# Second layer of an encoder: key and query weights, output-row squares, key spread and key scale at earlier places

## The chip, the core and the metric

The kernel runs on one core of a Trainium2 chip. The metric is the device time of one execution in microseconds (us), the median of several runs. The core has five engines that run side by side: PE (matrix products), DVE (vector work), ACT (activations and copies), POOL and SP. POOL and SP here mostly issue transfers: POOL those that convert or add on the way, SP plain ones.

## What is computed

A two-layer encoder over 1024 tokens of width 1024. In each layer a head group of latent attention runs beside a gated depthwise convolution of 31 taps; then comes a gated feed-forward block. The part that matters here:

```python
h = _rmsnorm(x, g_mix[l]);  p = h @ w_in[l]
c_q  = _rmsnorm(p[..., :384], g_q[l]);       q  = c_q @ w_uq[l]
c_kv = _rmsnorm(p[..., 384:640], g_kv[l]);   kv = c_kv @ w_ukv[l]
k_rope = _apply_rope(p[..., 640:672], cos, sin)
y_attn = _mla_attention(q_nope, q_rope, k_nope, k_rope, v)
u = a * sigmoid(gt);  u = _dwconv(u, w_dw_conv[l], b_dw_conv[l])
```

## The kernel before, in words

Everything is held transposed, 128 channels by 1024 tokens. A float32 factor is split into an upper and a lower part, and a product is made of three matmuls per half of the tokens (`product`, L252). `project` (L587) makes a layer's projections in sections: per section one block of 128 outputs in one of three wide places of PSUM. In the second layer the order is g0, a0, g1 (`next_sections`), then a1, g2, a2, g3, a3 (the convolution's gates), kv0, kv1 (key latent), kr (shared rope key), q0, q1, q2 (query latent), k0 to k3 (keys), u0, u1 (rope queries), n0 to n3 (queries).

The order on each engine is the order in which this code is written out; nothing is reordered later. `project` keeps a planned clock: `supply` (L922) asks for weights by the section's planned time, `out_squares` (L610) for rows of the output weights and their sum of squares, `work` (L635) emits queued steps of DVE and ACT, convolution taps among them, while the planned clock of DVE allows it. `start` (L665) emits a step's first part at once and queues the rest 1.8 us later on the planned clock.

Names that are needed below. `wk`, `wu2`, `wu0`, `wu1` are the weights of keys and queries, each an upper half (`h`, a converting transfer of POOL, L210) and a lower half (`l`: ACT writes the negated upper half, L225, and POOL adds the source to it, L226). `wor` are the output rows (SP L1043, squares by ACT L617). `hsq` is the square sum of `wk`. `far` tiles are scaled copies of the gate (ACT L2162) that POOL's transfers add into the convolution sums `conv` (L2163). `kss` is the key latent's sum of squares; `rkv1t` its transposes, `rkv1y` its inverse root (DVE L312 to L320), `rkv1s` the spread of that over the partitions (PE L339), `rkv` its copy (ACT L727). `keys_norm` (L724) scales the latent `ckv` by it and splits it into `kvs`, upper halves by ACT, lower by DVE (L785, L787). `kt` is a matmul that sums `qk` over the partitions; `key_scale` (L623) makes the keys' power-of-two scale from it, and `key_rope_end` (L769) the scaled rope key `krs`, which SP writes to memory as `krd`. `krt` is the rope key before that (L746). `cqs` are the split query latents, `qss` their sum of squares, `rq1y` the inverse root of that, `ks` the split keys.

Most of these tiles come from one pool, tag `b`, with 31 places of 4 KB per partition. A new tile gets a place that an older one had, and its first writer waits until the older tile's last user is done; for a `far` tile that is the landing of POOL's transfer.

Of the kernel before, what the change touches and what calls it, by code (L numbers as in the profile page):

```python
# [61 lines left out]
LEAD, TURN = 33.0, 22.0  # L62
# [62 lines left out]
BLOCKS = ("g0", "a0", "g1", "a1", "g2", "a2", "g3", "a3", "kv0", "kv1", "kr", "q0", "q1", "q2")  # L125
# [21 lines left out]
class Encoder:  # L147
# [102 lines left out]
                                           op0=ALU.mult, op1=ALU.subtract)  # L250
        return hi, lo

    def product(self, ps, weights, moving, by_half=False):
        nc = self.nc
        n = len(moving)
        for halves in ((0,), (1,)) if by_half else ((0, 1),):
            for k in range(n):
                (wh, wl), (xh, xl) = weights(k), moving[k]
                rest = ((wl, xh), (wh, xl)) if n <= 3 else ((wh, xl), (wl, xh))
                for s, (w, x) in enumerate(((wh, xh), *rest)):  # L260
                    for c in halves:
                        nc.tensor.matmul(ps[:, HALVES[c]], w, x[:, HALVES[c]], start=(k == 0 and s == 0),  # L262
                                         stop=(k == n - 1 and s == 2))
# [324 lines left out]
    def project(self, l, carry):  # L588
        nc, a = self.nc, self.a
        par = self.par[l]  # L590
        clock = {"pe": 0.0, "dve": 0.0}
        taps, active, u, conv, away, far_at = [], [], {}, {}, {}, {}
        gates, ckv, kvs, cq, cqs, vs, w = {}, [], [], [], [], [], {}
        heads, pending, spills = {}, {}, []
# [3 lines left out]
        krd = self.dp.tile([ROPE, 2, T], F16, name=f"krd{l}")  # L598
        qk = self.cp.tile([128, 8], F32, name=f"qk{l}", tag="qk", bufs=1)
        sc = self.cp.tile([128, 32], F32, name=f"sc{l}", tag="sc", bufs=1)  # L600
        outs = [(OUT_FROM + OUT_STEP * i, i, None) for i in range(4)]
        col = lambda i, n=1: qk[:, i:i + n]
        by = self.wz[:, 13:14]
        st = {}
# [18 lines left out]
        def key_scale():  # L623
            sums = self.bank(f"kt{l}", (128, 3))
            nc.tensor.matmul(sums, self.ones, col(4, 3), start=True, stop=True)
            nc.vector.tensor_copy(out=col(4, 3), in_=sums)
            nc.vector.scalar_tensor_tensor(out=col(4), in0=col(4), scalar=float(KVL), in1=col(5), op0=ALU.mult, op1=ALU.mult)
            nc.vector.tensor_tensor(out=col(4), in0=col(4), in1=col(6), op=ALU.add)
            self.half_exponent(col(5), col(4))
            self.power(col(6), col(5), -1.0, 200.0)  # L630
            self.power(col(2), col(5), 1.0, 54.0)
            nc.vector.tensor_scalar(out=col(2), in0=col(2), scalar1=SCALE, scalar2=None, op0=ALU.mult)
            launch(key_rope_end())

        def work(until):  # L635
            while True:
# [18 lines left out]
        def launch(steps, n=-1):  # L655
            active.append([clock["pe"], steps, n])
# [5 lines left out]
                    e[0] = clock["dve"] + step[1]  # L662
                active.remove(e)

        def start(steps):  # L665
            next(steps)
            active.append([clock["pe"] + 1.8, steps, 99])

        def gate(j):
            g = gates[j] = self.blk(f"gate{l}_{j}")  # L670
# [53 lines left out]
        def keys_norm():  # L724
            r = st["rkv"] = self.blk(f"rkv{l}")
            for s, p in zip(HALVES, self.spread(rooted("kroot"), f"rkv{l}", HALVES, self.bank)):
                nc.scalar.copy(out=r[:, s], in_=p)  # L727
            yield 0.0, 1.8
            for j in range(2):
                nc.vector.tensor_tensor(out=ckv[j], in0=ckv[j], in1=r, op=ALU.mult)  # L730
                yield 1.25, 0.0
            both = [parts(ckv[j], f"kvs{l}_{j}", kvs, par[:, P_GKV + j:P_GKV + j + 1]) for j in range(2)]
            yield [next(p) for p in both][0]
            for p in both:
                yield from p
# [34 lines left out]
        def key_rope_end():  # L770
            t, hl = st.pop("kr"), self.blk(f"krs{l}", F16, (128, 2, T))[0:32]
            by = qk[0:32, 6:7]
            nc.scalar.activation(out=hl[:, 0], in_=t, func=AF.Copy, scale=by)
            yield 0.0, 1.5
            nc.vector.scalar_tensor_tensor(out=hl[:, 1], in0=t, scalar=by, in1=hl[:, 0], op0=ALU.mult, op1=ALU.subtract)
            self.move(krd, hl)
            yield 1.25, 0.0

        def query_latent(j):
            yield from latent(f"q{j}", cq, "qss", j)  # L780
            yield from parts(cq[j], f"cqs{l}_{j}", cqs, par[:, P_GQ + j:P_GQ + j + 1])
# [70 lines left out]

        def inputs(name):
            if l:
                return lambda: self.product(ps[name], lambda k: (w[name][:, 0, k], w[name][:, 1, k]), hl)
            return lambda: self.product(ps[name], self.tiled(w[name]), hl)

        def ranked(group, j, n, name, moving):
# [5 lines left out]
        def root(key, out, n, name):  # L864
            ps = self.turned(st.pop(key), f"{name}{l}", HALVES, self.bank)

            def steps():
                st[out] = self.roots(ps, 8, n, f"{name}{l}")
                yield 2.5, 0.0

            pending[out] = [clock["pe"] + 2.0, steps(), 99]
            active.insert(0, pending[out])

        def rooted(out):
# [8 lines left out]
        add = lambda name, weight, emit, evict, after=None: seq.append((name, weight, emit, evict, after))  # L883
# [10 lines left out]
            add(f"kv{j}", f"kv{j}", inputs(f"kv{j}"), lambda j=j: latent(f"kv{j}", ckv, "kss", j))  # L894
        add("kr", "kr", shared_key, key_rope)
        add("q0", "q0", inputs("q0"), lambda: query_latent(0), lambda: root("kss", "kroot", KVL, "rkv"))
        add("q1", "q1", inputs("q1"), lambda: query_latent(1), lambda: (start(keys_norm()), key_scale()))
        add("q2", "q2", inputs("q2"), lambda: query_latent(2))
        between = {2 + l: lambda: root("qss", "qroot", QL, "rq")}
        norm = lambda: start(queries_norm())  # L900
# [15 lines left out]
        coming, turning = list(starts.items()) + [("v", t + 5.0)], []  # L916

        def rest_of(e):
            self.scaled_rest(*e)
            yield 1.28, 0.0  # L920

        def supply(now, turn=TURN):  # L922
            while coming and coming[0][1] <= now + LEAD:
                name, at = coming.pop(0)
                turning.append((name, at, self.cast(l, name)))
            while turning and turning[0][1] <= now + turn:
                name, at, e = turning.pop(0)
                if l and name in BLOCKS:
                    e = self.scaled(*e)
                    w[name] = e[0]  # L930
                    launch(rest_of(e), st.get("n", -3) - 2)
                    continue
                w[name] = self.complete(*e)
                if name == "k":
                    head_squares(name)

        hl, rx, ps = self.first_sections(l, supply) if l == 0 else self.next_sections(l, carry, supply)
# [146 lines left out]
    def wo_steps(self, l, conv, ys, w, casts, x, steps, put):  # L1084
# [14 lines left out]
        def load(i):  # L1099
            casts[i] = self.out_rows(l, i, "ws")  # L1100
# [1220 lines left out]
```

## Time and profile before

| | |
|---|---|
| median of 3 runs | 2173.98 us (2173.74 to 2175.91) |
| profiled execution | 2174.71 us, its span 2172.9 us |
| PE busy | 2160.1 us, 99% of the span |
| DVE, ACT, POOL busy | 86%, 68%, 24% |
| granted clock of PE, mean | 0.999 |

The profile is of one execution. Its span runs from the first instruction to the last; 1.8 us of the time lie outside. Times in rows are in us from the span's start. An engine takes its instructions strictly in order, so one that waits holds back all behind it. The sections of the change lie between 1140 and 1260 us.

### The profile page before, as it was taken

How to read it: one execution, taken by the hardware profiler on the slowest of the kernel's cores; microseconds unless marked ns; L12 is line 12 of the kernel's file. 1: busy time of each engine (PE TensorE's matmuls, PEld its weight loads, DVE VectorE, ACT ScalarE, POOL GpSimd, SP SyncE). 2: the span in 40 equal slices, each digit the busy share in tenths (PEclk: the TensorE clock that was granted, in tenths of full speed). 3: DMA queues.
4: the chain of work that ended last, by engine and by line, in shares of the span. 5: the costliest groups of instructions: out<-in, count | busy, mean ns of one | idle time of the engine just before them, and what ended most of it. 6: DMA issues, size and time to landing. Idle time of an engine off the chain costs nothing.

```text
span 2172.9 us, 29815 instructions
## 1 busy us (share of the span) xinstructions
PE 2160.1 (99%) x10726; PEld 1178.3 (54%) x10726; DVE 1859.4 (86%) x2558; ACT 1480.1 (68%) x2208; POOL 517.2 (24%) x506
## 2 busy tenths in 40 slices
PE   9999999999999999999999999999999999999998
PEld 8887666754444444444444576667544444444445
DVE  6989999879998887887978889998898988878877
ACT  6365888746898889554533768886478888865544
POOL 1232767211211111000000356771111111110000
PEclk9999999999999999999999999999999999999999
DMA  6898878854689898555334986786646988856533
GB/s 193 180 192 209 169 147 167 257 150 117 140 238 260 225 286 264 191 173 186 115 121 101 201 209 137 157 196 192 174 102 161 264 242 242 238 140 218 191 114 121
DMA packets 161220, 400.95 MB, mean 185 GB/s; under 512 B 19840, under 2 KB 27888, under 8 KB 161072
## 3 DMA queue, kind: packets, MB, share of 16 engines
q1 hardware_dynamic: 104080, 266.79, 35.8%
q0 software_dynamic: 56704, 131.74, 33.7%
q8 instruction: 84, 1.38, 0.3%
q10 hardware_dynamic: 288, 0.53, 0.1%
q14 instruction: 64, 0.52, 0.1%
HBM read 270.75 MB, written 69.66 MB: 157 GB/s over the span
## 4 chain that ended last, share of the span: by engine, by line
PE 93%; DVE 3%; ACT 2%; DMA 1%; issue 1%; DVEq 0%; SPq 0%; ACTq 0%
PE p L1376 36%; PE pd L1650 18%; PE po L1082 7%; PE s L1935 7%; PE t L1975 5%; PE pa L262 3%; PE o L1997 2%; PE pg L262 2%; PE pn L262 2%; PE pq L262 2%; PE pkv L262 1%; PE o L2002 1%; PE pg L585 1%; PE pv L1911 1%; PE pk L262 1%; DVE conv L2156 1%
## 5 line engine op out<-in xcount | busy, mean ns | idle before, releaser
L1376 PE MATMUL p<-b,w 128*128 128x512 f16 x3696 | 800.3, 379 | 0.3
L1376 PEld LDWEIGHTS <-w 128*128 128x128 f16 x3696 | 358.8, 98 | 431.7 <-issue 1.0
L1650 PE MATMUL pd<-ab,wd 128*128 128x512 f16 (+1 forms) x1920 | 401.0, 371 | 0.4 <-DVE ab L1640 0.4
L1252 POOL DMA_DIRECT2D wu<-in_w_up x176 | 152.5, 880 | 770.3 <-DVE w L1340 582.2
L1650 PEld LDWEIGHTS <-wd 128*128 128x128 f16 x1920 | 187.9, 98 | 210.7 <-issue 0.9
L1935 PE MATMUL s<-k,q 96*128 96x512 f16 x768 | 186.9, 379 | 0.0
L1340 DVE SCALAR_TENSOR_TENSOR w<-wu,wf,w 128x512 f16<-128x512 f32 (+1 forms) x216 | 177.3, 835 | 5.7 <-ACT w L1337 5.7
L1978 DVE SCALAR_TENSOR_TENSOR pt<-t,pt 128x512 f16<-128x512 f32 x256 | 163.0, 677 | 10.0 <-ACT pt L1977 9.0
L1337 ACT ACTIVATE w<-wu,wf 128x512 f16<-128x512 f32 (+1 forms) x216 | 165.2, 783 | 0.4 <-DMA wu<-in_w_up 0.4
L1977 ACT ACTIVATE pt<-t 128x512 f16<-128x512 f32 x256 | 139.2, 596 | 32.0 <-PE t L1975 30.0
L1937 DVE TENSOR_REDUCE mx<-s 128x1 f32<-128x1024 f32 x128 | 155.0, 1211 | 1.0 <-PE s L1935 1.0
L1639 ACT ACTIVATE ab<-ac,ds 128x512 f16<-128x512 f32 x108 | 75.6, 718 | 110.6 <-DVE ac L1545 73.6
L1945 ACT ACTIVATE p<-s,mx 128x1024 f32<-128x1024 f32 x128 | 143.3, 1120 | 2.3 <-DVE mx L1937 1.8
L2173 POOL TENSOR_SCALAR late<-gate,par 128x1012 f32<-128x1012 f32 (+14 forms) x99 | 135.8, 1372 | 27.4 <-PE pn L262 27.4
L2156 DVE SCALAR_TENSOR_TENSOR conv<-gate,par,conv 128x1009 f32<-128x1009 f32 (+14 forms) x110 | 139.7, 1274 | 2.8 <-ACT conv L688 0.2
L1975 PE MATMUL t<-ident,p 128*128 128x128 f32 x1024 | 136.6, 275 | 0.9 <-ACT p L1945 0.6
L1975 PEld LDWEIGHTS t<-ident,p 128*128 128x128 f32 x1024 | 116.8, 141 | 34.9 <-issue 8.2
L1883 DVE SCALAR_TENSOR_TENSOR o<-zg,par,o 128x1023 f32<-128x1023 f32 x88 | 112.8, 1282 | 10.0 <-ACT o L1877 8.4
L1883 DVE SCALAR_TENSOR_TENSOR v<-zv,par,v 128x1023 f32<-128x1023 f32 x88 | 112.2, 1277 | 1.4 <-ACT v L1877 1.4
L1384 DVE SCALAR_TENSOR_TENSOR zg<-p,wf,zg 128x512 f32<-128x512 f32 x72 | 54.0, 750 | 66.3 <-PE p L1376 52.7
L2163 POOL DMA_DIRECT2D conv<-far x31 | 26.5, 867 | 351.2 <-ACT far L2162 332.2
L1935 PEld LDWEIGHTS <-q 96*128 96x128 f16 x768 | 74.1, 97 | 64.5 <-issue 2.1
(1536 smaller groups left out, 3710.9 us busy)
## 6 DMA issues: line engine op xcount, KB each, us to landing
wu<-in_w_up SPq DMA_DIRECT2D x98, 512.0 KB
wu<-in_w_up POOLq DMA_DIRECT2D x176, 256.0 KB, 5.1
sd<-in_w_down SPq DMA_DIRECT2D x44, 512.0 KB
ws<-sd SPq DMA_DIRECT2D x44, 512.0 KB
act<-v SPq DMA_DIRECT2D x36, 512.0 KB
ac<-act SPq DMA_DIRECT2D x72, 256.0 KB
wo<-in_w_o POOLq DMA_DIRECT2D x32, 256.0 KB, 7.9
x_mix<-y SPq DMA_DIRECT2D x32, 256.0 KB
```

Source lines behind the costliest of these rows:

```text
L262: nc.tensor.matmul(ps[:, HALVES[c]], w, x[:, HALVES[c]], start=(k == 0 and s == 0), stop=(k == n - 1 and s == 2))
L1252: nc.gpsimd.dma_start(out=dst, in_=src, accum_op=ALU.add)
L1337: nc.scalar.activation(out=t, in_=src, func=AF.Copy, scale=scale[f])
L1340: nc.vector.scalar_tensor_tensor(out=t, in0=src, scalar=scale[f], in1=hi, op0=ALU.mult, op1=ALU.subtract)
L1376: nc.tensor.matmul(ps, w[p][:, k * 128:(k + 1) * 128], b[:, q], start=(i in (1, 5, 2) and k == 0 and t == 0), stop=(k == 3 and t == 2), sk ...
L1650: nc.tensor.matmul(ps[t, m][:, cs], w[i, j][p][:, m * 128:(m + 1) * 128], b[:, q, cs], start=(i in (1, 5, 2) and j == 0 and s == 0), stop= ...
L1883: self.nc.vector.scalar_tensor_tensor(out=o[:, a:b], in0=z[:, at + a:at + b], scalar=self.par[l][:, tap:tap + 1], in1=o[:, a:b], op0=ALU.m ...
L1935: nc.tensor.matmul(ps[:, cs], q[0:96, i, qs], k[0:96, j, cs], start=(s == 0), stop=(s == 2))
L1937: nc.vector.tensor_reduce(out=mx, in_=ps, op=ALU.max, axis=AX.X, negate=True)
L1975: nc.tensor.transpose(tp[:, i, qi * 128:(qi + 1) * 128], st["p"][2 * qp + qi][:, kt * 128:(kt + 1) * 128], self.ident)
L1978: nc.vector.scalar_tensor_tensor(out=lo, in0=tp, scalar=P_SCALE, in1=hi, op0=ALU.mult, op1=ALU.subtract)
L2156: self.nc.vector.scalar_tensor_tensor(out=y[:, lo:hi], in0=u[:, lo + s:hi + s], scalar=self.tap(l, j, t), in1=y[:, lo:hi], op0=ALU.mult, o ...
```

## The change

All of it concerns the second layer. (1) `supply` asks for `wk` and the `wu` weights 40 us sooner than before, past names that are still in the queue, and the `wu` tiles come from the pool `b` instead of `ws`. (2) The output rows start at a planned time of 6 us instead of 56. (3) The spread of the keys' inverse root and the matmul `kt` are emitted inside the product of section q1, before its fifth and its eighth slice, instead of behind it; the steps that follow are queued. (4) The inverse root may be taken 0.5 us after its sums on the planned clock instead of 2.0.

```diff
--- before.py
+++ after.py
@@ -74,6 +74,7 @@
 END_TURNS = 1
 SCALES_AT = 2, 4.2
 OUT_FROM, OUT_STEP, OUT_WAIT = 56.0, 10.0, 24.0
+OUT_NEXT, AHEAD = 6.0, 40.0
 WO_LOAD = (0, 1, 2, 3)
 WO_UPPER = (3, 2), (3, 2.1), (4, 2), (5, 2)
 WO_LOWER = (3, 4), (4, 2), (5, 2), (6, 2)
@@ -250,11 +251,13 @@
                                            op0=ALU.mult, op1=ALU.subtract)
         return hi, lo
 
-    def product(self, ps, weights, moving, by_half=False):
+    def product(self, ps, weights, moving, by_half=False, between={}):
         nc = self.nc
         n = len(moving)
         for halves in ((0,), (1,)) if by_half else ((0, 1),):
             for k in range(n):
+                if k in between:
+                    between[k]()
                 (wh, wl), (xh, xl) = weights(k), moving[k]
                 rest = ((wl, xh), (wh, xl)) if n <= 3 else ((wh, xl), (wl, xh))
                 for s, (w, x) in enumerate(((wh, xh), *rest)):
@@ -598,7 +601,7 @@
         krd = self.dp.tile([ROPE, 2, T], F16, name=f"krd{l}")
         qk = self.cp.tile([128, 8], F32, name=f"qk{l}", tag="qk", bufs=1)
         sc = self.cp.tile([128, 32], F32, name=f"sc{l}", tag="sc", bufs=1)
-        outs = [(OUT_FROM + OUT_STEP * i, i, None) for i in range(4)]
+        outs = [((OUT_NEXT if l else OUT_FROM) + OUT_STEP * i, i, None) for i in range(4)]
         col = lambda i, n=1: qk[:, i:i + n]
         by = self.wz[:, 13:14]
         st = {}
@@ -623,6 +626,7 @@
         def key_scale():
             sums = self.bank(f"kt{l}", (128, 3))
             nc.tensor.matmul(sums, self.ones, col(4, 3), start=True, stop=True)
+            yield 0.0, 0.0
             nc.vector.tensor_copy(out=col(4, 3), in_=sums)
             nc.vector.scalar_tensor_tensor(out=col(4), in0=col(4), scalar=float(KVL), in1=col(5), op0=ALU.mult, op1=ALU.mult)
             nc.vector.tensor_tensor(out=col(4), in0=col(4), in1=col(6), op=ALU.add)
@@ -631,6 +635,7 @@
             self.power(col(2), col(5), 1.0, 54.0)
             nc.vector.tensor_scalar(out=col(2), in0=col(2), scalar1=SCALE, scalar2=None, op0=ALU.mult)
             launch(key_rope_end())
+            yield 1.2, 0.0
 
         def work(until):
             while True:
@@ -662,9 +667,9 @@
                     e[0] = clock["dve"] + step[1]
                 active.remove(e)
 
-        def start(steps):
+        def start(steps, wait=1.8):
             next(steps)
-            active.append([clock["pe"] + 1.8, steps, 99])
+            active.append([clock["pe"] + wait, steps, 99])
 
         def gate(j):
             g = gates[j] = self.blk(f"gate{l}_{j}")
@@ -852,7 +857,8 @@
 
         def inputs(name):
             if l:
-                return lambda: self.product(ps[name], lambda k: (w[name][:, 0, k], w[name][:, 1, k]), hl)
+                between = {4: lambda: start(keys_norm(), 6.5), 7: lambda: start(key_scale(), 9.6)} if name == "q1" else {}
+                return lambda: self.product(ps[name], lambda k: (w[name][:, 0, k], w[name][:, 1, k]), hl, between=between)
             return lambda: self.product(ps[name], self.tiled(w[name]), hl)
 
         def ranked(group, j, n, name, moving):
@@ -868,7 +874,7 @@
                 st[out] = self.roots(ps, 8, n, f"{name}{l}")
                 yield 2.5, 0.0
 
-            pending[out] = [clock["pe"] + 2.0, steps(), 99]
+            pending[out] = [clock["pe"] + (0.5 if l else 2.0), steps(), 99]
             active.insert(0, pending[out])
 
         def rooted(out):
@@ -894,7 +900,7 @@
             add(f"kv{j}", f"kv{j}", inputs(f"kv{j}"), lambda j=j: latent(f"kv{j}", ckv, "kss", j))
         add("kr", "kr", shared_key, key_rope)
         add("q0", "q0", inputs("q0"), lambda: query_latent(0), lambda: root("kss", "kroot", KVL, "rkv"))
-        add("q1", "q1", inputs("q1"), lambda: query_latent(1), lambda: (start(keys_norm()), key_scale()))
+        add("q1", "q1", inputs("q1"), lambda: query_latent(1), None if l else lambda: (start(keys_norm()), list(key_scale())))
         add("q2", "q2", inputs("q2"), lambda: query_latent(2))
         between = {2 + l: lambda: root("qss", "qroot", QL, "rq")}
         norm = lambda: start(queries_norm())
@@ -919,12 +925,14 @@
             self.scaled_rest(*e)
             yield 1.28, 0.0
 
+        ahead = lambda name: AHEAD if l and name[0] in "ku" and name not in BLOCKS else 0.0
+
         def supply(now, turn=TURN):
-            while coming and coming[0][1] <= now + LEAD:
-                name, at = coming.pop(0)
-                turning.append((name, at, self.cast(l, name)))
-            while turning and turning[0][1] <= now + turn:
-                name, at, e = turning.pop(0)
+            for name, at in [e for e in coming if e[1] <= now + LEAD + ahead(e[0])]:
+                coming.remove((name, at))
+                turning.append((name, at, self.cast(l, name, "b" if ahead(name) and name != "k" else "ws")))
+            for name, at, e in [e for e in turning if e[1] <= now + turn + ahead(e[0])]:
+                turning.remove((name, at, e))
                 if l and name in BLOCKS:
                     e = self.scaled(*e)
                     w[name] = e[0]
```

In the change's order a line number is one to eight higher than before (L218 is now L219, L2162 is L2170).

**First place: ACT ahead of the rope key.** On ACT around the sections kr and q0 there stood before:

```order
L218 ACTIVATE wq1s_10547<-wq11r_10471,wz_75 128x1024 [waits DMAHW2_49]
L2162 ACTIVATE far1_2_16_10584<-gate1_2_10257,par1_155 128x1023 [waits DMASW2_49]
L218 ACTIVATE wq2s_10594<-wq21r_10545,wz_75 128x1024 [waits DMAHW4_49,DVE_49]
L2162 ACTIVATE far1_0_17_10647<-gate1_0_10052,par1_155 128x1022 [waits DMASW3_49]
L2162 ACTIVATE far1_1_17_10650<-gate1_1_10114,par1_155 128x1022 [waits DVE_49]
L2162 ACTIVATE far1_2_17_10653<-gate1_2_10257,par1_155 128x1022 [waits DMASW4_49]
L751 ACTIVATE krt1_10657<-pkr1_10551,wz_75 64x1024 [waits PE_49]
L763 COPY krt21_10664<-krt1_10657 32x1024 [waits DMASW5_49,DVE_49,Activation_49]
L766 ACTIVATE krt21_10664,qk1_9838<-krt1_10657 32x1024 [waits DVE_49]
```

And now:

```order
L219 ACTIVATE wq1s_10575<-wq11r_10492,wz_75 128x1024 [waits DMAHW6_49]
L226 ACTIVATE wu01l_10495<-wu01h_10494 128x768 [waits DMASW6_49]
L2170 ACTIVATE far1_2_16_10612<-gate1_2_10261,par1_155 128x1023 [waits DVE_49]
L219 ACTIVATE wq2s_10619<-wq21r_10570,wz_75 128x1024 [waits DMAHW7_49,DMASW0_49]
L226 ACTIVATE wu11l_10573<-wu11h_10572 128x768 [waits DMASW2_49,PE_49]
L2170 ACTIVATE far1_0_17_10672<-gate1_0_10052,par1_155 128x1022 [waits DMASW1_49]
L2170 ACTIVATE far1_1_17_10675<-gate1_1_10114,par1_155 128x1022 [waits DMASW4_49,Activation_49]
L2170 ACTIVATE far1_2_17_10678<-gate1_2_10261,par1_155 128x1022 [waits DVE_49]
L756 ACTIVATE krt1_10682<-pkr1_10579,wz_75 64x1024 [waits DMASW6_49,Activation_49]
L768 COPY krt21_10689<-krt1_10682 32x1024 [waits DVE_49,PE_49]
```

POOL's transfers report on eight counters in turn, DMASW0 to DMASW7. On POOL there now stand, in order:

```order
L211 DMA wu11h_10572<-in_w_uq 128x2x384 [waits DMAHW3_49,DMAHW6_49,DMASW2_49,DVE_49]
L227 DMA wu01l_10495<-in_w_uq 128x2x384 [waits DMAHW7_49,DMASW3_49,Activation_49]
L2171 DMA conv1_2_10331<-far1_2_16_10612 128x1023 [waits DMAHW1_49,DVE_49,Activation_49]
L227 DMA wu11l_10573<-in_w_uq 128x2x384 [waits DMAHW5_49,Activation_49]
L2171 DMA conv1_0_10112<-far1_0_17_10672 128x1022 [waits DMASW6_49,DMASW0_49,Activation_49]
L2171 DMA conv1_1_10179<-far1_1_17_10675 128x1022 [waits DMASW7_49,DMASW1_49,Activation_49]
L2171 DMA conv1_2_10331<-far1_2_17_10678 128x1022 [waits DMASW4_49,Activation_49]
L2171 DMA conv1_0_10112<-far1_0_18_10785 128x1021 [waits DMASW6_49,Activation_49]
L2171 DMA conv1_1_10179<-far1_1_18_10788 128x1021 [waits DMASW7_49,DMASW2_49,Activation_49]
L2171 DMA conv1_2_10331<-far1_2_18_10791 128x1021 [waits DMASW3_49,DMASW0_49,Activation_49]
```

The lower halves of `wu0` and `wu1` stand between the far copies now. Counting from `wu11h`, whose landing ACT's `wu11l` awaits on DMASW2, the transfer of `far1_2_16` is DMASW4 and that of `far1_0_17` DMASW6. So `far1_1_17` now waits for the landing of `far1_2_16`, and `krt1`, which waited for PE before, for that of `far1_0_17`: `far1_1_17` has the place that `far1_2_16` had, `krt1` the place of `far1_0_17`.

**Second place: ACT behind the root's spread.** Before, from the far copies to the rope key's end:

```order
L2162 ACTIVATE far1_0_18_10742<-gate1_0_10052,par1_155 128x1021
L2162 ACTIVATE far1_1_18_10745<-gate1_1_10114,par1_155 128x1021 [waits PE_49]
L2162 ACTIVATE far1_2_18_10748<-gate1_2_10257,par1_155 128x1021 [waits DMASW1_49]
L785 ACTIVATE cqs1_0h_10751<-cq01_10679,par1_155 128x1024
L727 COPY rkv1_10772<-rkv1s_10773 128x512 [waits PE_49]
L727 COPY rkv1_10772<-rkv1s_10778 128x512 [waits PE_49]
L709 ACTIVATE cq11_10794<-pq11_10693,wz_75 128x1024 [waits Activation_49]
L719 ACTIVATE qss1_1_10796<-cq11_10794 128x1024 [waits Activation_49]
L225 ACTIVATE wu21l_10684<-wu21h_10683 128x768 [waits DMASW2_49]
L617 ACTIVATE wor1_1b_10549,sc1_9839<-wor1_1b_10549 128x1024 [waits DMAHW5_49]
L773 ACTIVATE krs1_10804<-krt1_10657,qk1_9838 32x1024 [waits DMASW4_49,DVE_49]
```

And now:

```order
L732 COPY rkv1_10733<-rkv1s_10747 128x512 [waits PE_49]
L732 COPY rkv1_10733<-rkv1s_10752 128x512 [waits PE_49]
L2170 ACTIVATE far1_0_18_10785<-gate1_0_10052,par1_155 128x1021 [waits DMASW0_49]
L2170 ACTIVATE far1_1_18_10788<-gate1_1_10114,par1_155 128x1021 [waits DMASW5_49]
L2170 ACTIVATE far1_2_18_10791<-gate1_2_10261,par1_155 128x1021
L790 ACTIVATE cqs1_0h_10794<-cq01_10704,par1_155 128x1024 [waits DMASW1_49,Activation_49]
L790 ACTIVATE kvs1_0h_10802<-ckv01_10488,par1_155 128x1024 [waits DMASW2_49,DVE_49,Activation_49]
L790 ACTIVATE kvs1_1h_10805<-ckv11_10566,par1_155 128x1024 [waits DVE_49,Activation_49]
L778 ACTIVATE krs1_10815<-krt1_10682,qk1_9838 32x1024 [waits DMASW3_49,DVE_49]
```

The spread's copies stand ahead of the far copies now, and the upper halves `kvs` ahead of `krs`. `cqs1_0h`, `kvs1_0h` and `krs1` wait for the landings of `far1_0_18`, `far1_1_18` and `far1_2_18` (DMASW1, 2 and 3).

**Third place: DVE from the rope key's end to the first keys.** Before:

```order
L775 SCALAR_TENSOR_TENSOR krs1_10804<-krt1_10657,qk1_9838,krs1_10804 32x1024 [waits DMASW4_49,DMASW0_49,Activation_49]
L730 TENSOR_TENSOR ckv01_10467<-ckv01_10467,rkv1_10772 128x1024
L730 TENSOR_TENSOR ckv11_10541<-ckv11_10541,rkv1_10772 128x1024
L280 SCALAR_TENSOR_TENSOR qss1_10681<-qss1_10681,qss1_1_10796 128x1024 [waits DMASW7_49,DMASW3_49]
L2156 SCALAR_TENSOR_TENSOR conv1_3_10459<-gate1_3_10389,par1_155,conv1_3_10459 128x1021
L787 SCALAR_TENSOR_TENSOR kvs1_0l_10869<-ckv01_10467,par1_155,kvs1_0h_10868 128x1024 [waits PE_49,Activation_49]
L787 SCALAR_TENSOR_TENSOR kvs1_1l_10872<-ckv11_10541,par1_155,kvs1_1h_10871 128x1024 [waits Activation_49]
L787 SCALAR_TENSOR_TENSOR cqs1_1l_10876<-cq11_10794,par1_155,cqs1_1h_10875 128x1024 [waits DMASW1_49,Activation_49]
L2156 SCALAR_TENSOR_TENSOR conv1_3_10459<-gate1_3_10389,par1_155,conv1_3_10459 128x1022 [waits DVE_49]
L799 SCALAR_TENSOR_TENSOR ks1_0_10922<-pk01_10892,qk1_9838,ks1_0_10922 128x1024 [waits Activation_49]
```

And now:

```order
L780 SCALAR_TENSOR_TENSOR krs1_10815<-krt1_10682,qk1_9838,krs1_10815 32x1024 [waits DMASW3_49,Activation_49]
L792 SCALAR_TENSOR_TENSOR kvs1_0l_10803<-ckv01_10488,par1_155,kvs1_0h_10802 128x1024 [waits DMAHW0_49,DVE_49]
L792 SCALAR_TENSOR_TENSOR kvs1_1l_10806<-ckv11_10566,par1_155,kvs1_1h_10805 128x1024 [waits PE_49]
L283 SCALAR_TENSOR_TENSOR qss1_10706<-qss1_10706,qss1_1_10819 128x1024 [waits DMASW4_49,Activation_49]
L2164 SCALAR_TENSOR_TENSOR conv1_3_10480<-gate1_3_10402,par1_155,conv1_3_10480 128x1019
L2164 SCALAR_TENSOR_TENSOR conv1_3_10480<-gate1_3_10402,par1_155,conv1_3_10480 128x1020 [waits DVE_49]
L792 SCALAR_TENSOR_TENSOR cqs1_1l_10885<-cq11_10817,par1_155,cqs1_1h_10884 128x1024 [waits Activation_49]
L2164 SCALAR_TENSOR_TENSOR conv1_3_10480<-gate1_3_10402,par1_155,conv1_3_10480 128x1021 [waits DVE_49]
L2164 SCALAR_TENSOR_TENSOR conv1_3_10480<-gate1_3_10402,par1_155,conv1_3_10480 128x1022 [waits DVE_49]
L804 SCALAR_TENSOR_TENSOR ks1_0_10924<-pk01_10894,qk1_9838,ks1_0_10924 128x1024 [waits DMASW5_49,Activation_49]
```

`kvs1_0l` now waits on DMAHW0, which is the landing of SP's `krd`, since it has the place of `krs1`. Between `kvs1_1l` and `ks1_0` there stand four taps of `conv1_3` and the addition to `qss`, where one tap stood.

## Rows read from the trace of the kernel before

**Rows 1.** The page, chain that ended last: shares of the span by engine
```profile
PE 93%; DVE 3%; ACT 2%; DMA 1%; issue 1%; DVEq 0%; SPq 0%; ACTq 0%
```

**Rows 2.** Who PE waited for in the whole run: us in total, times, longest
```profile
PE pk L262 <- DVE kvs_0l L787: 1.8, 1, 1.8
```

**Rows 3.** PE in order of time: start us, us, what [idle before]
```profile
1209.41 10.52 PE L262 MATMUL pq<-xs,wq1s 128*128 128x512 f16 x48
...
1221.83 0.38 PE L625 MATMUL kt<-qk,ones_r 128*128 128x3 f32 x2 [1.03 <-ACT rkv L727]
...
1235.62 0.73 PE L262 MATMUL pk<-kvs_0l,wk1h 128*128 128x512 f32 x2 [1.76 <-DVE kvs_0l L787]
...
1251.11 1.06 PE L339 MATMUL rq1s<-ident,rq1y 128*128 128x128 f32 x8 [0.26 <-DVE rq1y L317]
```

**Rows 4.** The chain in order of time: start us, us, what
```profile
1235.62 10.27 PE pk L262 x44
```

**Rows 5.** ACT in order of time
```profile
1195.08 1.13 ACT L218 ACTIVATE wq1s<-wq11r,wz 128x1024 f16<-128x1024 f32 x1
...
1198.20 3.22 ACT L2162 ACTIVATE far<-gate,par 128x1022 f32<-128x1022 f32 x3
...
1201.44 1.11 ACT L751 ACTIVATE krt<-pkr,wz 64x1024 f32<-64x1024 f32 x1
...
1224.27 0.83 ACT L225 ACTIVATE wu21l<-wu21h 128x768 fp32r<-128x768 f32 x1
```

**Rows 6.** DVE in order of time
```profile
1204.48 1.27 DVE L753 SCALAR_TENSOR_TENSOR krt<-pkr,wz,krt 64x1024 f32<-64x1024 f32 x1
...
1209.52 1.21 DVE L765 TENSOR_TENSOR krt<-krt,krt 32x1024 f32<-32x1024 f32 x1
...
1211.84 1.27 DVE L312 TENSOR_REDUCE rkv1v<-rkv1t 128x4 f32<-128x512 f32 x2
...
1214.36 0.17 DVE L317 SCALAR_TENSOR_TENSOR rkv1y<-rkv1q,rkv1y 128x8 f32<-128x8 f32 x1
...
1221.35 1.28 DVE L787 SCALAR_TENSOR_TENSOR cqs_0l<-cq,par,cqs_0h 128x1024 fp32r<-128x1024 f32 x1 [6.82 <-ACT cqs_0h L785]
...
1222.55 3.91 DVE L2156 SCALAR_TENSOR_TENSOR conv<-gate,par,conv 128x1018 f32<-128x1018 f32 x3
...
1229.70 2.34 DVE L730 TENSOR_TENSOR ckv<-ckv,rkv 128x1024 f32<-128x1024 f32 x2
```

**Rows 7.** POOL's transfers issued 1185:1189, 1199:1200.5, 1200.5:1202, 1218:1219.2; last: us to landing
```profile
conv<-far POOLq DMA_DIRECT2D x1, 511.5 KB, 4.6
...
conv<-far POOLq DMA_DIRECT2D x1, 511.0 KB, 8.2
...
conv<-far POOLq DMA_DIRECT2D x1, 511.0 KB, 9.6
...
conv<-far POOLq DMA_DIRECT2D x1, 510.5 KB, 6.1
```

**Rows 8.** SP's issue of krd; its queue's packets in 1231.5:1233.2 (count, MB, share)
```profile
1229.80 0.33 SPq L155 DMA_DIRECT2D krd<-krs  x1
...
q1 hardware_dynamic: 48, 0.13, 20.1%
```

**Rows 9.** Busy time in stretches: us, PE, PEld, DVE, ACT, POOL, PEclk, DMA, GB/s
```profile
2168.00:2170.00 2.00, 0.00 (x0) 0.00 (x0) 0.75 (x2) 0.47 (x1) 0.00 (x0) 1.00 0.68 240
...
2170.50:2171.00 0.50, 0.00 (x0) 0.00 (x0) 0.00 (x0) 0.00 (x0) 0.00 (x0) 0.50 1.03 385
```

**Rows 10.** PE at the run's start, in order of time
```profile
1.06 3.78 PE L453 MATMUL warm<-ones_r 128*128 128x128 f32 x16 [1.06 <-DVE ones_r L428]
...
5.91 0.63 PE L537 MATMUL pg<-xs_0l,wg00h 128*128 128x512 f32 x1
...
6.34 0.43 PE L537 MATMUL pa<-xs_0l,wa00h 128*128 128x512 f32 x1
```

**Rows 11.** Who ACT waited for in 1119:1260: us in total, times, longest
```profile
ACT conv L688 <- DVE gate L684: 23.3, 3, 8.6
```

## The prediction

> **What bounds the kernel now.** I read the page's chain first: 93% of the span hangs on PE [rows 1]. So a change counts only where PE stands still, or is made to. Then I asked who PE waited for: the longest wait of the whole run is 1.8 us in the first key section, for DVE's `kvs_0l` [rows 2]. PE's own order of time shows the three waits that the change can touch [rows 3]: 1.03 us before `kt`, 1.76 us in k0, 0.26 us before `rq1s`, together 3.05 us. That is all there is to win, 0.14% of the time. A measurement of this kernel can tell some 0.2% (4.3 us) from no change.
>
> Why are they there? DVE stands idle for 6.82 us until ACT's `cqs_0h` is done [rows 6], and behind it come three taps, the scale and `ckv`, only then `kvs_0l`. The change takes the output rows and lower weight halves off ACT there and starts the spread earlier, so on paper all three waits go. I then looked at what the moved work now waits for.
>
> **The change part by part.** *Earlier requests and squares.* Four square sums and the lower halves of the weights go to ACT between 1140 and 1200. There ACT waited 23.3 us for DVE's gates in three waits alone [rows 11], and each of the moved instructions takes about 1 us; they cost PE nothing up to the rope key. Without that cover they would delay the gates, some 1 us apiece. SP issues the rope tables behind the first output row, long before `krt` uses them: nothing.
>
> *First stall, the spread inside q1.* The order shows that `krt1` now waits for the landing of `far1_0_17`, and everything behind it on ACT with it. Step by step:
> - ACT starts `wq1s` at 1195.08, and one 1024-wide instruction follows another every 1.04 us (three from 1195.08 to 1198.20) [rows 5]. A lower half of `wu` takes 0.83 us [rows 5], 0.1 less as a step. So `wu01l` starts at 1196.1, `far1_2_16` at 1196.9, `wq2s` at 1197.9, `wu11l` at 1198.9, and `far1_0_17` is done at 1200.8.
> - POOL issues the four transfers at 1197.0, 1198.0, 1199.8 and 1200.8. From an idle queue one lands after 4.6 us [rows 7]. Behind others it lands later: two far copies that ACT makes 1.04 us apart landed 8.2 and 9.6 us after their issue [rows 7], so 2.4 us apart. That gives 1201.6, 1204.0, 1206.4 and 1208.8.
> - `far1_1_17` must wait until 1204.0, and `krt1` starts at 1208.8 instead of 1201.44 [rows 5], 7.4 us late.
> - From there to `rkv1y`: ACT 1.11 [rows 5], three DVE steps like 1.27 with their gaps 3.8, ACT's copy 1.1, DVE's addition 1.21, then reduction and root, 1211.84 to 1214.53, 2.7 [rows 6]. In all 10.0 us: 1218.8.
> - PE starts q1 at 1209.41 and needs about 10.4 us for its 48 matmuls [rows 3], so it reaches the spread, before the fifth of eight slices, at 1214.6. **It stands 4.2 us.**
>
> *Second stall, k0.* PE then has the spread (0.9), the rest of q1 (5.2), `kt` (0.25), q2 (10.4) and four matmuls of k0 (0.9): it asks for `kvs1_0l` at 1236.4. On the other side the rope key's addition is done at 1216.1; ACT squares it, evicts q0 and squares that (3.4 us, 1219.5), copies the spread when PE has made it (1220.9) and makes `far1_0_18` (1222.0). Now `cqs1_0h` waits for the landing of that: plus 4.6, 1226.6. Then ACT 1.1 and DVE 1.28 for `cqs1_0l` (1229.0), `ckv` 2.34 [rows 6] (1231.3); ACT's `kvs1_0h`, `kvs1_1h`, `krs1` end at 1233.5, DVE's half of `krs1` at 1234.8. `kvs1_0l` has the place of `krs1` and must wait until SP's `krd` has landed. SP's queue shows `krd` issued at 1229.80 and its 48 packets in 1231.5 to 1233.2 [rows 8]; I take 3.6 us. 1238.4, and `kvs1_0l` is done at 1239.7. **PE stands 3.3 us.**
>
> *Third stall, k3.* k3 takes the PSUM place of k0, so it waits for DVE's `ks1_0`. From `kvs1_0l` on DVE has `kvs1_1l`, `qss`, two taps, `cqs1_1l`, two taps, `ks1_0`: eight steps of 1.2 to 1.3 (three taps take 3.91 [rows 6]), 9.8 us, to 1249.5. PE needs 32 matmuls of 0.23 (44 in 10.27 [rows 4]), 7.3 us, to 1247.0. **PE stands 2.5 us.** Before, only one tap stood there and this wait did not exist.
>
> *Queries' root.* Behind `ks1_0` DVE has five steps of 1.2 and the root (2.7): 1258.2. PE has k3, the transposes and u0 (7.6): 1257.1. I take 0.8 us for the 0.26 of before.
>
> *Sum.* 4.2 + 3.3 + 2.5 + 0.8 = 10.8 us of new standing, less 3.05 that goes: plus 7.7 us. From k3 on nothing gives it back: attention and what follows hang on PE [rows 1]. The profiled execution would be 2182.4; it stood 0.7 above the median, so I say **2181.7**.
>
> *Bounds.* The uncertain size is the landing of POOL's transfers. From below: `far1_0_17` lands 4.6 us after its own issue, as from an idle queue, at 1205.4; then the first stall is 0.8, and the sum plus 4.3, 2178.3. From above: the first transfer of each group takes 6.1, as one did behind an idle stretch [rows 7]; then each of the first two stalls grows by 1.5, plus 10.7, 2184.7. I take the 4.6 because `far1_0_16` had it under the same conditions.
>
> The Trainium skill's page DMA: Bandwidth & Descriptors, section Anatomy of one DMA, gives such a transfer about 2.0 us and its bytes by 436 GB/s. My estimate from that page is 3.2 us for 512 KB; the rows show nothing under 4.6. By the page's figure the first stall would vanish and the sum would be near plus 2.
>
> **Rivals.**
> - *Landings sooner than reckoned.* For it speaks that the weights' loads, which filled the queue at 1198 to 1204 before, now come earlier. Against it: two weight transfers stand right between the far copies. If the queue is as good as idle, 2178.3 as above; if a landing takes still less, down to some 2176, since the third stall stays: it is DVE's order alone. Chance 0.18.
> - *The clock falls in a stall.* The granted clock was full to 2170 with PE idle from 2168 at the latest, and at half, 1.2 instead of 2.4 GHz, from 2170.5 [rows 9]; so standing as long as the first stall could halve it. At the start PE's first matmul came at 1.06, and at 6.34 they were still 0.43 apart [rows 10] against 0.23 later [rows 4]: some 5.4 us at half rate, 2.7 us lost. One such fall gives 2184.4, two 2187.1. Against it: nothing in the middle of this run shows a fall, and the mean clock is whole there. The Trainium skill's TensorE: Matmul & The Clock Gate, section HAM oscillation, says that a wait for a transfer can leave PE with the lower clock when it resumes. By that rule the 2.7 us would come at the first stall at least; the end of the run agrees that idleness lowers it. Chance 0.18.
> - *It goes as written, not slower.* The place where it is decided is `krt1`: with 10.0 us from there to `rkv1y`, PE never waits if `far1_0_17` has landed by 1204.6, 3.8 us after its issue, and the far copies of 18 likewise. Then `kvs1_0l` comes some 3 us before PE asks, all three waits go, and the time is 2174.0 - 3.05 = 2170.9. Against it stands every landing in the rows. Chance 0.08; it includes the case that the pool's places do not bind at all.
>
> **How the numbers follow.** The forecast has 0.56 (2179.5 to 2184.5), the clock 0.18 (to 2187), sooner landings 0.18 (2176 to 2178.5), the gain 0.08. The range 2176.5 to 2186.5 leaves out the gain, the lower end of the sooner landings and the worst of the clock, under 0.2. Slower by over 0.2% is over 2178.3: forecast, clock, and some 0.04 of the sooner landings, 0.78. Within 0.2%: the rest of these and most of the gain, which is under the bound, 0.19. Faster by over 0.2%: 0.03.
>
> **What would show it.** In the profile of the changed kernel: ACT's `krt` waits for a transfer of `conv` and starts near 1209; PE has a wait of about 4 us for `rkv1y` inside q1, one of about 3 us for `kvs_0l` in k0, one of about 2.5 us for `ks` at k3; `kt` has none. The prediction is wrong if `krt` starts before 1204.6, if PE finds `kvs_0l` ready, or if a later stage returns the lost time. A granted clock under 1.00 between 1215 and 1250 would show the second rival.

## The result and the profile after

The changed kernel takes 2182.55 us, the median of 6 runs (2181.26 to 2183.59), beside 2174.48 for the kernel before in 6 runs: ratio 1.0036, 95% interval 1.0023 to 1.0049. It is slower by some 8 us. The profiled execution took 2182.62 us, its span is 2180.8 where it was 2172.9.

PE in order of time (start, us, what, idle before it and for whom), to be read beside [rows 3]:

```profile
1208.92 5.34 PE L265 MATMUL pq<-xs,wq1s 128*128 128x512 f16 x24
1219.88 1.94 PE L342 MATMUL rkv1s<-ident,rkv1y 128*128 128x128 f32 x8 [5.62 <-DVE rkv1y L320]
1221.62 5.62 PE L265 MATMUL pq<-xs,wq1s 128*128 128x512 f16 x18
1227.08 0.28 PE L628 MATMUL kt<-qk,ones_r 128*128 128x3 f32 x2
...
1239.34 0.63 PE L265 MATMUL pk<-kvs_0h,wk1l 128*128 128x512 f32 x2
1240.75 0.73 PE L265 MATMUL pk<-kvs_0l,wk1h 128*128 128x512 f32 x2 [0.78 <-DVE kvs_0l L792]
...
1250.49 0.73 PE L265 MATMUL pk<-kvs_0h,wk1h 128*128 128x512 f32 x2 [2.13 <-DVE ks L804]
...
1259.09 1.06 PE L342 MATMUL rq1s<-ident,rq1y 128*128 128x128 f32 x8 [0.61 <-DVE rq1y L320]
```

The wait before `kt` is gone and that in k0 is 0.78 instead of 1.76 us, but a stall of 5.62 us stands inside q1, and one of 2.13 at k3. From q1's first matmul to `rq1s`, the spread of the queries' root, it is 50.17 us; before, 1209.41 to 1251.11 is 41.70 [rows 3]. That is 8.47 more, and the span grew by 7.9 (PE came to q1 0.49 earlier): all of the loss lies here, and nothing later returns it.

ACT in order of time shows why, beside [rows 5]:

```profile
1199.33 0.85 ACT L226 ACTIVATE wu11l<-wu11h 128x768 fp32r<-128x768 f32 x1 [0.79 <-DMA wu11h<-in_w_uq]
1200.08 1.13 ACT L2170 ACTIVATE far<-gate,par 128x1022 f32<-128x1022 f32 x1
1204.49 2.18 ACT L2170 ACTIVATE far<-gate,par 128x1022 f32<-128x1022 f32 x2 [3.28 <-DMA conv<-far]
1209.72 1.11 ACT L756 ACTIVATE krt<-pkr,wz 64x1024 f32<-64x1024 f32 x1 [3.04 <-DMA conv<-far]
```

`krt` starts at 1209.72 instead of 1201.44, behind two waits for landings. The chain that ended last (start, us, what) goes through the same transfer:

```profile
1201.78 7.86 DMA conv<-far
```

The stretches of the profile (start:end, length, busy us of PE, PEld (its weight loads), DVE, ACT, POOL with counts, then PE's granted clock, DMA share, GB/s) show what the stall did to PE:

```profile
1214.00:1217.00 3.00, 0.27 (x2) 0.00 (x0) 2.97 (x3) 1.04 (x1) 0.00 (x0) 1.00 0.00 0
1217.00:1219.80 2.80, 0.00 (x0) 0.00 (x0) 2.56 (x11) 2.58 (x4) 0.00 (x0) 0.67 0.00 0
1219.80:1221.00 1.20, 1.12 (x6) 1.15 (x7) 1.17 (x2) 0.74 (x1) 0.00 (x0) 0.50 0.00 0
...
1224.00:1225.00 1.00, 1.00 (x4) 0.38 (x3) 0.00 (x0) 1.00 (x2) 0.82 (x2) 0.60 0.00 0
1225.00:1226.00 1.00, 1.00 (x7) 0.41 (x5) 0.00 (x0) 0.56 (x1) 0.82 (x2) 1.00 1.00 184
```

While PE stands, the granted clock falls from 1.00 to 0.50 (1.2 of 2.4 GHz); it is 1.00 again from 1225. In between the spread takes 1.74 us from start to start (0.87 in the run wu_ws below), and 18 matmuls of q1 take 5.46 where at 10.4 for 48 they take 3.9: 2.4 us lost. The four stalls, 9.14 us, and the 2.4, less the 3.05 of before, make 8.5, the 8.47 that were lost.

### The profile page after: what moved, and what is told of

Its sections match the earlier page's. It is cut to its first block, busy times and chain, and to the rows that moved or that the text cites. A ratio compares the mean times of both kernels' runs of the same rounds, so it can differ in the third digit from the quotient of the medians.

```text
span 2180.8 us, 29822 instructions
## 1 busy us (share of the span) xinstructions
PE 2162.5 (99%) x10726; PEld 1179.4 (54%) x10726; DVE 1859.5 (85%) x2558; ACT 1479.8 (68%) x2208; POOL 515.7 (24%) x506
## 4 chain that ended last, share of the span: by engine, by line
PE 93%; issue 2%; DVE 2%; ACT 2%; DMA 1%; POOL 0%; DVEq 0%; POOLq 0%; ACTq 0%
PE p L1384 36%; PE pd L1658 18%; PE po L1090 7%; PE s L1943 7%; PE t L1983 5%; PE pa L265 3%; PE o L2005 2%; PE pg L265 2%; PE pg L588 2%; PE pn L265 2%; PE pq L265 2%; PE o L2010 1%; PE pv L1919 1%; PE pkv L265 1%; PE pa L588 1%
```

## The experiments

The theory: the new tiles of `wu` in pool `b` make its places scarce, so that the rope key and its neighbours take places whose last user is a far copy's transfer, and wait for the landing. The rivals: the earlier transfers and copies themselves are in the way; or the spread inside q1 is. Each run (4 to 11 executions) is compared with runs of the kernel before on the same chip: their median was 2174.91 us for the first four rows of the table, 2175.62 for the next four and 2175.24 for the last two, beside 2174.48 for the change. So a difference of about 1 us between runs of different groups says little by the medians alone.

| run | what it has | median us | ratio (95% interval) |
|---|---|---|---|
| wu_ws | whole change, `wu` in `ws` | 2170.76 | 0.9981 (0.9972 to 0.9990) |
| far_wr | whole change, far copies in `wr` | 2172.61 | 0.9989 (0.9980 to 0.9998) |
| spread_only | spread and scale in q1 | 2177.49 | 1.0012 (1.0003 to 1.0020) |
| early_only | weights and rows | 2180.35 | 1.0026 (1.0015 to 1.0037) |
| krs_m | whole change, `krs` in `m` | 2181.38 | 1.0029 (1.0018 to 1.0039) |
| q1_twice | whole change, PE kept working in the stall | 2180.45 | 1.0024 (1.0014 to 1.0034) |
| weights_only | weights | 2202.24 | 1.0125 (1.0111 to 1.0139) |
| rows_only | rows | 2174.44 | 0.9996 (0.9987 to 1.0005) |
| ws_early | weights and rows, `wu` in `ws` | 2171.71 | 0.9984 (0.9975 to 0.9993) |
| rows_spread | rows, spread and scale | 2178.11 | 1.0012 (1.0004 to 1.0021) |

**Places or load: wu_ws and far_wr.** Each is the whole change with one line changed:

```diff
-                turning.append((name, at, self.cast(l, name, "b" if ahead(name) and name != "k" else "ws")))
+                turning.append((name, at, self.cast(l, name, "ws")))
```

```diff
-        p = self.blk(f"far{l}_{j}_{t}") if l else self.tmp("wr", f"far{l}_{j}_{t}")
+        p = self.tmp("wr", f"far{l}_{j}_{t}") if l else self.tmp("wr", f"far{l}_{j}_{t}")
```

> The change whole, with its earlier weights, squares, spread and key scale; only the tiles of wu2, wu0 and wu1 come from the pool ws again. Transfers, copies and matmuls are the same in number and nearly the same in order. Theory (the places of pool b cost the time, by the landings that new tiles wait for): krt starts near 1201.5, as before the change, no instruction of ACT waits for a far copy's landing there, PE has under 0.5 us of waits between 1200 and 1262, and all three old waits are gone: 2174.5 - 3.1 = 2171.4 us. Rival (the earlier transfers and ACT's earlier copies are themselves in the way): krt stays late and PE stands over 5 us, 2179 to 2183 us.

> The change whole; only the second layer's far copies come from the three places of pool wr instead of pool b. Theory (places): a far copy waits for the landing of the third far copy before it, and krt for none. The copy of tap 17 for group 2 then still waits for that of tap 16, so krt starts some 2 us later than before the change; PE stands about 0.5 us at the spread in q1 and nowhere else over 0.3: 2174.5 - 2.7 = 2171.8 us. Rival (load of the transfers, whatever the places): 2179 to 2183 us.

PE of wu_ws, its only wait in these sections, and ACT's `krt`:

```profile
1214.25 1.04 PE L342 MATMUL rkv1s<-ident,rkv1y 128*128 128x128 f32 x8
...
1247.10 1.06 PE L342 MATMUL rq1s<-ident,rq1y 128*128 128x128 f32 x8 [0.26 <-DVE rq1y L320]
```

```profile
1203.39 1.11 ACT L756 ACTIVATE krt<-pkr,wz 64x1024 f32<-64x1024 f32 x1
```

PE of far_wr:

```profile
1216.30 1.06 PE L342 MATMUL rkv1s<-ident,rkv1y 128*128 128x128 f32 x8 [1.61 <-DVE rkv1y L320]
...
1249.20 1.06 PE L342 MATMUL rq1s<-ident,rq1y 128*128 128x128 f32 x8 [0.26 <-DVE rq1y L320]
```

Where the tiles of three tensors lie is worth some 12 us (1.0036 to 0.9981). All transfers, copies and steps are as early as in the change, so the load is not what costs.

wu_ws is faster than both kernels: `rq1s` comes 4.01 us sooner than before, and its span of 2168.9 is 4.0 shorter. The waits of [rows 3] less the 0.26 that stays make 2.79 of it, and PE's earlier start of q1 0.34. Of the other 0.9, 0.4 is a wait that the view does not list: before, k0 starts at 1232.67, right behind ACT's `kvs_0h` (1231.49, 1.13 long), 10.59 us after q2's first matmul, where 10.17 pass in wu_ws; the rest lies in no one place. `krt` came 1.9 us later than expected, behind the lower halves and a wait of 0.72 for `wu11h`, and PE did not feel it.

far_wr stands 1.1 us longer than expected at the spread, since the copy that waits for tap 16's landing starts at 1204.96.

**Which part: spread_only, early_only.**

```diff
-OUT_NEXT, AHEAD = 6.0, 40.0
+OUT_NEXT, AHEAD = 56.0, 0.0
```

(without AHEAD the `wu` tiles come from `ws`); and for early_only

```diff
-                between = {4: ...} if name == "q1" else {}
+                between = {4: ...} if name == "none" else {}
...
-        add("q1", ..., None if l else lambda: (start(keys_norm()), list(key_scale())))
+        add("q1", ..., lambda: (start(keys_norm()), list(key_scale())))
...
-            pending[out] = [clock["pe"] + (0.5 if l else 2.0), steps(), 99]
+            pending[out] = [clock["pe"] + 2.0, steps(), 99]
```

> Only the spread and the key scale inside q1, with the shorter wait of the root; weights and output rows as before. Theory (the spread's place costs nothing by itself, what is late is the rope key): krt starts near 1201.4, PE does not wait at the spread, nor for kt or kvs_0l; but DVE now has four taps and qss ahead of ks1_0, and ACT the upper half of ks1_0 behind later work, so PE stands about 3.5 us at k3 and some 1.6 us in three smaller waits: 5.2 - 3.5 us, 2176.1 us. Rival one (the spread inside q1 is what costs): a stall of about 5 us at rkv1y, 2180 us or more. Rival two (this part gives what it is for): 2171.5 us.

> Only the weights and the output rows earlier, with wu in pool b; spread and key scale behind q1 as before. Theory (places): krt is as late as in the change, 1209 to 1210; PE meets that behind q1: about 0.4 us at the spread, 5 us at kt and 1.3 us in k0, no wait at k3: 7.1 - 3.5 us, 2178.0 us; up to 2 us more where the clock falls at kt. Rival (only the spread inside q1 makes the lateness count, behind q1 there is slack enough): within 1 us of before, 2173.5 to 2175.5 us.

Who PE waited for (total us, times, longest), first spread_only, then early_only:

```profile
PE pk L265 <- DVE ks L804: 3.2, 1, 3.2
PE rq1s L342 <- DVE rq1y L320: 0.7, 1, 0.7
PE pk L265 <- ACT cq L714: 0.4, 1, 0.4
```

```profile
PE kt L628 <- ACT rkv L732: 5.3, 1, 5.3
PE rkv1s L342 <- DVE rkv1y L320: 1.2, 1, 1.2
```

ACT's `krt` in early_only, then a stretch of spread_only and one of early_only:

```profile
1209.30 1.11 ACT L756 ACTIVATE krt<-pkr,wz 64x1024 f32<-64x1024 f32 x1 [2.60 <-DMA conv<-far]
```

```profile
1240.00:1250.00 10.00, 6.80 (x26) 5.36 (x27) 6.25 (x6) 6.48 (x8) 1.80 (x3) 0.83 1.08 238
```

```profile
1220.00:1230.00 10.00, 4.03 (x17) 2.16 (x18) 5.97 (x11) 7.41 (x9) 2.57 (x3) 0.76 0.77 145
```

The spread alone meets its data (no wait at `rkv1s`) and loses its gain at k3, as reckoned. The earlier weights and rows carry the late `krt` without any spread in q1. Both are slower than expected, by 1.4 and 2.4 us; for early_only up to 2 of that were allowed for a lower clock. In both the clock falls, as the stretches show: it is granted 0.83 in 1240 to 1250 in spread_only, behind the wait of 3.2 us, and 0.76 in 1220 to 1230 in early_only, in and behind that of 5.3.

**Weights and rows apart: weights_only, rows_only.** early_only with OUT_NEXT = 56.0, and with AHEAD = 0.0.

> Only the weights earlier, with wu in pool b; output rows, spread and key scale as before. Theory (places): the output rows now hold their places while the far copies and the rope key need some, so places are scarcer than with both: krt is at 1211 to 1212, the tile rkv has the place of cq0 and waits until cqs_0l is made, which itself waits for a landing; PE stands about 3 us at the spread, 13 us at kt, 7 us in k0 and 2.5 us later: 25.9 - 3.5 = 22.4 us, 2197 us, and up to 5 more where the clock falls. Rival (the weights' load on POOL and ACT, with less of it than in weights and rows together): not over the 2180.4 us of weights and rows together.

> Only the output rows and their squares earlier; all else as before. Theory: no tile of the rope key or the keys gets another's place with a landing to wait for; kt's wait falls from 1.0 to 0.4 us, the wait in k0 stays near 1.8: 1.0 us less than before, 2173.9 us. Rival (the rows' transfers or squares are part of the loss): over 2176 us.

Who PE waited for in weights_only, and ACT there:

```profile
PE kt L628 <- ACT rkv L732: 13.1, 1, 13.1
PE pk L265 <- ACT kvs_0h L790: 4.8, 1, 4.8
PE rkv1s L342 <- DVE rkv1y L320: 3.6, 1, 3.6
```

```profile
1207.95 0.84 ACT L226 ACTIVATE wu11l<-wu11h 128x768 fp32r<-128x768 f32 x1 [7.26 <-DMA conv<-far]
...
1237.76 1.07 ACT L732 COPY rkv<-rkv1s 128x512 f32<-128x512 f32 x2 [3.77 <-DVE cqs_0l L792]
```

The weights alone cost 26.6 us, five times what they cost with the earlier rows (5.4), though less is moved: the load alone would make them cost less, the theory of places said 22.4 and up to 5 for the clock. The reason that the order of the code gives is that a row holds its place until it is squared; no run takes this apart. The rows alone can't be told from no change; the wait in k0 is still 1.76.

**The second stall and the clock: krs_m, q1_twice.**

```diff
-        t, hl = st.pop("kr"), self.blk(f"krs{l}", F16, (128, 2, T))[0:32]
+        t, hl = st.pop("kr"), self.tmp("m" if l else "b", f"krs{l}", F16, (128, 2, T))[0:32]
```

```diff
                 if k in between:
+                    if k == 4:
+                        for i in range(4):
+                            (wh, wl), (xh, xl) = weights(i), moving[i]
+                            for s, (w, x) in enumerate(((wh, xh), (wh, xl), (wl, xh))):
+                                for c in halves:
+                                    nc.tensor.matmul(ps[:, HALVES[c]], w, x[:, HALVES[c]], start=False, stop=False)
                     between[k]()
```

> The change whole; only the scaled rope key krs has a place in pool m, so kvs_0l no longer has the place of krs and needs no landing of krd. Theory: kvs_0l starts when DVE has finished krs, some 2 us earlier; the 0.8 us in k0 goes, ks1_0 is 2 us earlier while PE is there 0.8 us earlier, so the wait at k3 falls from 2.1 to 0.9 us; the stall at the spread stays 5.6 us: 2182.6 - 2.0 = 2180.6 us. Rival (kvs_0l is late for ckv and not for krd): 2182.5 us.

> The change whole; before the spread PE adds the first four slices of q1 to q1's sums once more, 24 matmuls, 5.2 us, so that it works while it would stand (the values of q1 are another's then, the steps of all other engines the same). rkv1y is done at 1219.7 as before. Theory (standing lowers the granted clock, and the clock's price is mostly hidden by the second stall, since kvs_0l hangs on ACT's far copies and POOL's landings): the granted clock is 1.00 throughout, the half of q1 behind the spread takes 3.9 us for 18 matmuls instead of 5.5 and the spread 0.9 less, but the wait in k0 grows from 0.8 to some 2.3 us: 2182.6 - 0.9 = 2181.7 us. Rival one (the clock's price counts in full): 2182.6 - 2.4 = 2180.2 us. Rival two (the lower clock does not come from standing): the clock falls at the same place, 2182.6 us.

DVE's `kvs_0l` in the change and in krs_m, then PE, its waits and two stretches in q1_twice:

```profile
1239.41 1.28 DVE L792 SCALAR_TENSOR_TENSOR kvs_0l<-ckv,par,kvs_0h 128x1024 fp32r<-128x1024 f32 x1 [2.05 <-DMA krd<-krs]
```

```profile
1238.23 1.28 DVE L792 SCALAR_TENSOR_TENSOR kvs_0l<-ckv,par,kvs_0h 128x1024 fp32r<-128x1024 f32 x1 [1.37 <-PE pq L265]
```

```profile
1214.67 5.34 PE L265 MATMUL pq<-xs,wq1s 128*128 128x512 f16 x24
1220.09 1.06 PE L348 MATMUL rkv1s<-ident,rkv1y 128*128 128x128 f32 x8
1220.98 4.05 PE L271 MATMUL pq<-xs,wq1s 128*128 128x512 f16 x18
...
1224.87 0.28 PE L634 MATMUL kt<-qk,ones_r 128*128 128x3 f32 x2
```

```profile
PE pk L271 <- ACT cq L720: 1.2, 1, 1.2
PE pk L271 <- DVE ks L810: 0.7, 1, 0.7
PE rq1s L348 <- DVE rq1y L326: 0.7, 1, 0.7
PE pk L271 <- DVE kvs_0l L798: 0.4, 1, 0.4
```

```profile
1218.00:1220.00 2.00, 2.00 (x10) 0.69 (x8) 1.76 (x9) 1.94 (x4) 0.00 (x0) 1.00 0.00 0
1220.00:1225.00 5.00, 4.93 (x29) 2.90 (x29) 2.41 (x2) 4.93 (x6) 1.66 (x2) 1.00 0.13 25
```

In krs_m the wait for `krd` is gone, but `kvs_0l` now has the place of a tile that q2's matmuls read, and waits for those; the wait in k0 goes, that at k3 is 1.7. So 1.2 us are won by the medians, which are of different chips, and 1.1 at `rq1s` in the traces (1258.02 for 1259.09), where 2.0 were expected; the intervals of the two ratios overlap.

In q1_twice the clock is 1.00 throughout and the 18 matmuls take 3.9 us from start to start: standing is what lowered it. The time fell by 2.1 us, by the medians and at `rq1s` alike, near rival one's, but not for its reason alone: the added matmuls also gave `kvs_0l` another place, behind q2 as in krs_m.

Against krs_m, which shares that and was run on the same chip, the working PE is worth 0.93 us by the medians and 0.99 from q1's first matmul to `rq1s` in the traces (1209.49 to 1256.99, and 1209.53 to 1258.02), not 2.4; the intervals of the two ratios overlap. The rest came back as waits: PE, earlier now, stands 1.19 us until ACT has evicted q2, and 0.45 in k0, where krs_m has neither. ACT's second copy of the spread ends 2.57 us after the spread begins in krs_m and 1.73 in q1_twice; that share of the slower clock delays ACT too, and it is near what was won, which is an argument and no test. For the change's own places the clock's price was not measured apart.

**What the gain needs: ws_early, rows_spread.** early_only with the line of wu_ws, and the change with AHEAD = 0.0.

> Weights and output rows earlier with the wu tiles in pool ws, spread and key scale behind q1 as before the change: the run early_only with the places changed and nothing else. Theory (places): krt starts near 1203 as in the run wu_ws; kt waits 0.4 us, PE finds kvs_0l ready: 3.5 - 0.6 = 2.9 us under before, 2171.9 us, so the earlier weights and rows alone bring most of the gain. Rival (the gain of the run wu_ws is the spread's): 2174 us or more.

> The change without the earlier weights (their tiles in ws, asked for as before). Theory: krt starts near 1201, no wait for the spread, kt and kvs_0l; the lower half of wu0 or wu1 and the keys on ACT and DVE come together behind k1, so PE stands 3.3 us at u0 for ks1_1's place and 0.8 at rq1s: 4.1 - 3.5 = 0.6 us over before, 2175.3 us; the run spread_only had 5.2 us of waits by the same sum. Rival (the earlier weights only cost, the rows and the spread give the gain): 2172 us or less.

Who PE waited for in ws_early, and ACT of rows_spread:

```profile
PE rq1s L342 <- DVE rq1y L320: 0.3, 1, 0.3
PE kt L628 <- ACT rkv L732: 0.2, 1, 0.2
PE pk L265 <- DVE kvs_0l L792: 0.2, 1, 0.2
```

```profile
1246.68 0.84 ACT L226 ACTIVATE wu11l<-wu11h 128x768 fp32r<-128x768 f32 x1 [7.40 <-DMA wu11h<-in_w_uq]
```

Against early_only, ws_early changes only the places: 8.6 us by the medians, 0.0042 by the ratios. The earlier weights and rows bring most of the gain by themselves, and the spread in q1 adds about 1 us to it (wu_ws), which two intervals that overlap do not prove. Without the earlier weights the spread makes things worse: `wu11h`, issued among far copies, lands late, ACT stands 7.40 us for it, and behind it PE stands 4.5 at u0. I had reckoned 3.3 there, no wait at k3 (1.6 came) and a whole clock (0.57 in 1250 to 1255); the median is 2.8 us over what was expected. The profiled execution, 2180.0 us, is the longest of the 11, so these waits are those of a long one.

## Why the prediction was right, and where it was off

- **The place of the loss and its cause**: right. `krt` was forecast at 1208.8 and came at 1209.72; from it to `rkv1y` 10.0 us were reckoned and 10.02 came. The first stall was 5.62 instead of 4.2. The landing of `far1_0_17` was sized rightly, 7.86 us from its issue for 8.0; but the issue came at 1201.78 instead of 1200.8. ACT was done with that copy at 1201.21, 0.4 late: it began 0.49 sooner, but had to wait 0.79 us for `wu11h`, which I had not counted. POOL issued it 0.57 later still, behind the transfer of `wu11l`; the sum had put nothing between copy and issue. And PE was there 0.3 sooner.
- **The second rival came too**: the clock fell in the first stall and cost PE 2.4 us; 2.7 were reckoned. (That figure came from the spacing of the first matmuls of the run; the granted clock reads 1.00 from 0 to 8 us, so that the clock was lower there is not shown.) That the price would be added to the sum was that rival's wrong step: `kvs_0l` was done at 1240.7 (forecast 1239.7) by ACT's and POOL's chain, and PE, slowed, asked for it at 1240.0 instead of 1236.4. So the second stall was 0.78 instead of 3.3: most of the clock's price was taken out of the next stall, and the sum came out at 2182.6 instead of that rival's 2184.4. The comparison of q1_twice and krs_m points the same way.
- **The number is nearer than its terms**, in part by luck. 10.8 us of standing were forecast at a whole clock; 9.14 of standing and 2.4 of slower clock came. The term that was mis-sized is k0, 3.3 for 0.78, since PE came 3.6 us later than reckoned. `kvs_0l` was only 1.0 late because two errors met: `cqs_0h` started at 1229.03 instead of 1226.6, and DVE stood 2.05 us for the landing of `krd` where 3.6 were taken. With 3.6 the time would have been up to 1.5 us longer, an estimate from these rows.
- **The upper bound** took 6.1 us as a landing behind an idle stretch. It was not: when that copy was issued, at 1218.50, the transfer of `wk1l`, issued at 1215.38, was under way. The result lies inside all the same.
- **Third stall and root**: 2.13 and 0.61 for 2.5 and 0.8, right.
- **The two rules cited**: By the Trainium skill's page DMA: Bandwidth & Descriptors, Anatomy of one DMA, my estimate for a far copy was 3.2 us. The two far copies in the view below took 6.6 and 7.9, and the two weights, which are smaller, 5.2 and 6.1, so the measurement decides. The rule of the Trainium skill's TensorE: Matmul & The Clock Gate, HAM oscillation, that a wait for a transfer can leave PE with the lower clock, held in the first stall: the granted clock was 0.50 when PE resumed.
- **The rival that nothing binds** was wrong only by the places: wu_ws is that case, with 2170.76 where 2170.9 was given. That it is so near is chance too: 0.26 of the 3.05 stays, and the 0.9 above was not reckoned.

The transfers issued from 1197 to 1202.9 (KB each, us to landing):

```profile
conv<-far POOLq DMA_DIRECT2D x1, 511.5 KB, 6.6
conv<-far POOLq DMA_DIRECT2D x1, 511.0 KB, 7.9
wu01l<-in_w_uq POOLq DMA_DIRECT2D x1, 384.0 KB, 5.2
wu11l<-in_w_uq POOLq DMA_DIRECT2D x1, 384.0 KB, 6.1
```

## What to carry to other kernels

Where tiles come from one ring of places, a longer life of one tile moves the wait to whatever takes the next place: look up, for each tile on the critical engines' way, whose last use it follows, above all if that is a transfer's landing. Before giving up a prefetch that loses, give its tiles places of their own. And do not add the price of a slower clock to a sum in which another engine's chain sets the next wait.

## What was not expected

Moving less cost more: the weights alone 26.6 us, with the rows 5.4, with the rows and the spread 8.1. For the weights alone the expectation of that run said so; nothing in the prediction had. And a small edit elsewhere changed which place a tile got (krs_m, q1_twice), so that an experiment on one wait brought another.
